# A two-layer hybrid decoder on one core: a fourth pair by seven products in the MLP, low parts and down sums by adding DMAs, the residual kept in HBM, linear attention's products in runs

## The chip, the cores and the metric

One core of one Trainium2 chip runs the whole program. The metric is device time in microseconds, the median of several runs. The engines are TensorE (PE), VectorE (DVE), ScalarE (ACT), GpSimd (POOL) and SyncE (SP), each with its own queue of instructions in a fixed order; 16 DMA engines serve transfers that SP or GpSimd issue.

## The reference

Two layers on x of 256 rows and 2048 columns, all in float32. Each layer is

```python
h = rms_norm(x, attn_norm)
proj = jnp.einsum('bsd,de->bse', h, w_in)
...
mixed = jnp.concatenate([o_gla, o_sb], axis=-1)
x = x + jnp.einsum('bse,ed->bsd', mixed, w_o)
hm = rms_norm(x, mlp_norm)
up = jnp.square(jax.nn.relu(jnp.einsum('bsd,df->bsf', hm, w_up)))
return x + jnp.einsum('bsf,fd->bsd', up, w_down)
```

The projection feeds two groups of heads, eight heads of gated linear attention (`o_gla`) and eight of stick-breaking attention (`o_sb`). The linear attention works on four chunks of 64 rows: per head and chunk there is a state update `u = k_dec^T v` of 64 by 128, scores of 64 by 64 under a causal mask, an output `scores v` within the chunk and `q_e S` from the state of the chunks before. The MLP goes from 2048 to 8192 columns and back.

## The kernel before

**Float32 by three products.** Every weight tile arrives by DMA as `raw`. ScalarE copies it to a rounded high part (`whi`), VectorE subtracts to get the low part (`wlo`), and a float32 product is three matmuls on TensorE: high by high, low weight by high operand, high weight by low operand. Operands have such parts too. A matmul has 512 columns.

**The MLP** (and the output projection and one more column group before it) is cut into units: `g`, two `o`, then for each quarter q of the 8192 columns two `up` units and two `down` units of 1024 output columns each, so 16 MLP units in a layer and 32 in all. A unit has eight pairs j of two k-tiles; one pair is one load of 1 MB (SP, four buffers) and a product of 2 by 2 blocks (two row tiles, two halves of 512 columns, two k-tiles). A plain pair takes eight block products of three matmuls. A pair for which `fast(j)` holds (1, 3 and 5) takes seven, by sums of the weight's blocks (`ts`, `t`, made by VectorE) and of the operand's blocks (`sx`, `sxh`). The products land in eight PSUM banks m: 2, 4, 3 and 8 hold what plain pairs add, 1, 5, 6 and 7 what the seven products add besides. Five high parts and five low parts are in flight (`RING`); the next one in the ring takes the buffer of the one five before.

**Ends of units.** `up_tail` joins the banks, applies relu, turns the result round on TensorE, squares it and makes the operand's parts for the down unit. `down_tail` adds the banks to the residual `xb` in SBUF, twelve steps of 512 columns on VectorE and one copy on ScalarE in each down unit.

**The order.** `Plan` holds pieces with a length, an engine and what they depend on. TensorE's and SP's pieces stay in the order of the code; those of ScalarE and VectorE are sorted by a due time from their users, in a simulated run. The result is a fixed order of each engine.

**Linear attention** (`gla_pair`, `gla_out`) does its small products between the projection's matmuls: state updates (L971, 64 rows of the tile), scores (L988), outputs within the chunk (L1012, 128 rows) and from the state (L1024).

## Time and profile before

| | |
|---|---|
| median of three runs | 2185.33 us (2184.94 to 2186.03) |
| profiled execution | 2184.75 us |
| its span, first to last instruction | 2183.0 us |
| TensorE, VectorE, ScalarE, GpSimd busy | 100%, 85%, 58%, 2% of the span |
| DMA queue of SP | 407 MB, 57.0% of 16 engines |

In the profile's rows the letters after the line number name the engine, `out<-in` the tiles by the program's names; L1263 to L1265 are the three matmuls of one MLP product, L1172 the high parts, L1176 the low parts, L1052 every sum of two tiles on VectorE, L543 to L545 the matmuls of the projection. The attention of the first layer ends at about 300 us, its MLP at about 1070, the second layer has the rest.

### The profile page before, as it was taken

Reading aid. Unit: us, or ns where it says so; the run is one execution under the profiler, and the core shown is the slowest. Engines: PE = TensorE matmul, PEld = TensorE weight load, DVE = VectorE, ACT = ScalarE, POOL = GpSimd, SP = SyncE. Lnnn points to the kernel's source line nnn. Section 1 sums busy time; section 2 is a strip of 40 time slices with the busy share of each in tenths; the row PEclk is TensorE's granted clock in tenths of the full one; section 3 lists DMA queues with packets and bytes.
Section 4 is the critical chain, followed back from the end, with each engine's and each line's share of the span. In section 5 each row is a group of like instructions: output and inputs, shape, how many; then the busy total and the mean of one; then the engine's idle time right before and its main releaser. Section 6 shows DMA issues by size and latency. Waiting matters only on the chain.

```text
span 2183.0 us, 27194 instructions
## 1 busy us (share of the span) xinstructions
PE 2175.0 (100%) x10352; PEld 1803.6 (83%) x10352; DVE 1851.7 (85%) x2394; ACT 1276.6 (58%) x1659; POOL 38.0 (2%) x64
## 2 busy tenths in 40 slices
PE   9999999999999999999999999999999999999999
PEld 7988778888888888888888887788888888888887
DVE  5777568999999999999957775799999999999998
ACT  5555356665566566466556553666665655665663
POOL 0020000000000000000000200000000000000000
PEclk9999999999999999999999999999999999999999
DMA  6644455566556556655546544555656665565564
GB/s 230 198 155 155 154 175 191 164 209 206 193 193 212 185 200 198 208 193 193 174 156 196 171 154 154 174 175 191 214 174 211 199 204 193 193 212 186 199 199 149
DMA packets 144359, 408.98 MB, mean 187 GB/s; under 512 B 6650, under 2 KB 31810, under 8 KB 144228
## 3 DMA queue, kind: packets, MB, share of 16 engines
q1 hardware_dynamic: 144228, 407.24, 57.0%
q8 instruction: 81, 1.33, 0.2%
q14 instruction: 50, 0.41, 0.1%
HBM read 405.12 MB, written 2.10 MB: 187 GB/s over the span
## 4 chain that ended last, share of the span: by engine, by line
PE 99%; DVE 1%; DMA 0%; issue 0%; ACT 0%; SPq 0%; POOL 0%; ACTq 0%
PE acc L543 6%; PE acc L544 6%; PE acc L545 6%; PE acc L590 3%; PE acc L594 1%; PE ps L1012 1%; PE ps L1024 1%; PE ps L971 0%; PE ps L708 0%; PE ps L654 0%; PE ps L672 0%; DVE wlo L1176 0%; PE ps L988 0%; DMA raw<-in_w_in_dram 0%; PE ps L435 0%
## 5 line engine op out<-in xcount | busy, mean ns | idle before, releaser
L1172 ACT ACTIVATE whi<-raw 128x1024 fp32r<-128x1024 f32 x592 | 616.1, 1057 | 349.0 <-ACT whi L1172 11.6
L1176 DVE TENSOR_TENSOR wlo<-raw,whi 128x1024 fp32r<-128x1024 f32 x592 | 715.5, 1218 | 90.9 <-ACT whi L1172 85.7
L526 DVE TENSOR_TENSOR wlo<-raw,whi 128x1024 fp32r<-128x1024 f32 (+2 forms) x194 | 220.1, 1139 | 131.5 <-ACT whi L524 131.1
L524 ACT ACTIVATE whi<-raw 128x1024 fp32r<-128x1024 f32 (+2 forms) x194 | 189.8, 982 | 207.2 <-PE acc L545 158.1
L543 PE MATMUL acc<-whi,act 128*128 128x512 f32 (+2 forms) x640 | 242.3, 379 | 0.4 <-ACT act L445 0.4
L545 PE MATMUL acc<-whi,act 128*128 128x512 f32 (+2 forms) x640 | 237.0, 370 | 0.0
L544 PE MATMUL acc<-wlo,act 128*128 128x512 f32 (+2 forms) x640 | 236.9, 370 | 0.0
L1172 ACT ACTIVATE whi<-t 128x512 fp32r<-128x512 f32 x104 | 65.6, 631 | 162.2 <-DVE t L1052 154.2
L543 PEld LDWEIGHTS acc<-whi,act 128*128 128x128 f32 x640 | 120.9, 189 | 23.2 <-issue 4.1
L545 PEld LDWEIGHTS acc<-whi,act 128*128 128x128 f32 x640 | 120.6, 188 | 20.7 <-DVE act L451 0.2
L544 PEld LDWEIGHTS acc<-wlo,act 128*128 128x128 f32 x640 | 120.8, 189 | 18.9 <-issue 0.7
L1176 DVE TENSOR_TENSOR wlo<-ts,whi 128x1024 fp32r<-128x1024 f32 x104 | 127.1, 1222 | 7.1 <-ACT whi L1172 6.1
L1172 ACT ACTIVATE whi<-ts 128x1024 fp32r<-128x1024 f32 x104 | 109.6, 1054 | 35.1 <-PE m__2487_12202 L1265 2.1
L1052 DVE TENSOR_TENSOR ts<-raw 128x1024 f32<-128x1024 f32 x104 | 126.8, 1219 | 1.4
L590 PE MATMUL acc<-act,whi 128*128 128x512 f32 x256 | 91.9, 402 | 0.0
L1176 DVE TENSOR_TENSOR wlo<-t,whi 128x512 fp32r<-128x512 f32 x104 | 70.9, 682 | 2.8 <-ACT whi L1172 2.8
L594 PE MATMUL acc<-act,wlo 128*128 128x256 f32 x256 | 71.8, 280 | 0.0
L1052 DVE TENSOR_TENSOR raw<-ts,raw 128x512 f32<-128x512 f32 x104 | 70.9, 682 | 0.1
L1052 DVE TENSOR_TENSOR t<-raw 128x512 f32<-128x512 f32 x104 | 70.9, 682 | 0.1
L1349 ACT ACTIVATE act<-act,st 128x512 f32<-128x512 f32 x64 | 44.3, 717 | 26.5 <-DVE act L1052 26.5
L590 PEld LDWEIGHTS acc<-act,whi 128*128 128x128 f32 x256 | 48.1, 188 | 11.1
L594 PEld LDWEIGHTS acc<-act,wlo 128*128 128x128 f32 x256 | 48.4, 189 | 0.1
(2748 smaller groups left out, 5169.2 us busy)
## 6 DMA issues: line engine op xcount, KB each, us to landing
raw<-in_w_up_dram SPq DMA_DIRECT2D x128, 1024.0 KB, 5.0
raw<-in_w_down_dram SPq DMA_DIRECT2D x128, 1024.0 KB, 5.2
raw<-in_w_in_dram SPq DMA_DIRECT2D x84, 1024.0 KB, 5.2
raw<-in_w_o_dram SPq DMA_DIRECT2D x32, 1024.0 KB, 5.3
raw<-in_w_in_dram SPq DMA_DIRECT2D x14, 512.0 KB, 6.5
raw<-in_w_in_dram SPq DMA_DIRECT2D x8, 544.0 KB, 3.8
out_dram<-xb SPq DMA_DIRECT2D x8, 256.0 KB, 3.2
xb<-in_x_dram SPq DMA_DIRECT2D x3, 512.0 KB, 7.9
```

The lines of the kernel that those rows point to most:

```text
L524: newest["hi"] = nc.scalar.activation(h, r, AF.Copy).ins
L526: newest["lo"] = nc.vector.tensor_tensor(lo[:, q : q + step, :width], r, f32(h), ALU.subtract).ins
L543: nc.tensor.matmul(o, xh[:, sl], whi[:, j, :width], start=first, stop=False)
L544: nc.tensor.matmul(o, xh[:, sl], wlo[:, j, :width], start=False, stop=False)
L545: st["mm"] = nc.tensor.matmul(o, xl[:, sl], whi[:, j, :width], start=False, stop=last).ins
L590: nc.tensor.matmul(acc[f], whi[:, j, sl], op.both(k), start=(k == 0), stop=False, skip_group_check=True,)
L594: nc.tensor.matmul(acc[f][:, T:], wlo[:, j, sl], xh, start=False, stop=(k == KT - 1), skip_group_check=True,)
L1012: nc.tensor.matmul(o, sc[:, (2 * tt + j) * P : (2 * tt + j + 1) * P], v[:, tt, vc + j * P : vc + (j + 1) * P], start=first, stop=False, sk ...
L1052: nc.vector.tensor_tensor(dst, a, b, op)
L1172: nc.scalar.activation(box["h"][:, :n], src(), AF.Copy)
L1176: nc.vector.tensor_tensor(box["l"][:, :n], src(), f32(box["h"][:, :n]), ALU.subtract)
L1349: nc.scalar.activation(box[h][:, tt, :], box[h][:, tt, :], AF.Relu, scale=rr[:, tt : tt + 1],)
```

## The change

Four things are changed together.

1. In up and down units four pairs (kind F: 1, 3, 4, 6) go by seven products where there were three; two (kind P: 2, 7) stay plain; two (kind D: 0 and 5) are plain products with the low part made in another way. For D, ScalarE makes the high part of one k-tile (128 by 1024) in a tile `side` and copies it negated into another, and GpSimd issues a DMA that adds the weights from HBM once more to the negated part, which leaves the low part. There are two pairs of `side` tiles. Pair 0 of each layer's first up unit is still made by VectorE.
2. In the down units of the first three quarters the banks are not summed into `xb`: ScalarE copies them, VectorE makes three differences, and GpSimd issues nine DMAs of 256 KB that add the tiles to the residual in HBM, one behind the other where they go to the same columns (`add_tail`).
3. The residual lies in the output tensor in HBM. It is stored after the output projection, loaded into tiles of the activation pool for the last quarter, whose down units sum as before, stored again, and in the second layer loaded on SP at the 20th step of the attention. `side` uses the four residual tiles in the meantime. Masks, a scan's reset row, gate weights and zeroed keys move to a pool of the attention's own and are built again in the second layer.
4. In linear attention the six state products come in one run and the VectorE steps behind them; the four outputs within the chunk come first and then the six from the state.

GpSimd is a fifth engine of the planner, sorted by due times as ScalarE and VectorE are.

```diff
+    KINDS = "DFPFFDFP"
+
     def fast(i):
-        return i in (1, 3, 5)
+        return KINDS[i] == "F"
 
...
             pu = ps_tile()
             S = tmp("S", [P, 3, P], bufs=3)
             for n in range(3):
-                u = pu[:, n * P : (n + 1) * P]
                 for half in range(2):
                     ps = slice(half * DK, (half + 1) * DK)
                     nc.tensor.matmul(
-                        u[ps, :], kdz["t"][:, n, e * P + half * DK : e * P + (half + 1) * DK],
+                        pu[ps, n * P : (n + 1) * P],
+                        kdz["t"][:, n, e * P + half * DK : e * P + (half + 1) * DK],
                         v[:, n // 2, vc + half * P : vc + (half + 1) * P],
                         start=(n == 0), stop=True, skip_group_check=True,
                     )
-                if n == 0:
-                    nc.vector.tensor_copy(S[:, 0, :], u)
-                else:
-                    nc.vector.scalar_tensor_tensor(
-                        S[:, n, :], S[:, n - 1, :], dec[:, e, n : n + 1], u,
-                        ALU.mult, ALU.add,
-                    )
+            nc.vector.tensor_copy(S[:, 0, :], pu[:, :P])
+            for n in range(1, 3):
+                nc.vector.scalar_tensor_tensor(
+                    S[:, n, :], S[:, n - 1, :], dec[:, e, n : n + 1],
+                    pu[:, n * P : (n + 1) * P], ALU.mult, ALU.add,
+                )
...
+            for i, (tt, j) in enumerate((tt, j) for tt in range(NT) for j in range(2)):
+                nc.tensor.matmul(
+                    block(j, tt), sc[:, (2 * tt + j) * P : (2 * tt + j + 1) * P],
+                    v[:, tt, vc + j * P : vc + (j + 1) * P],
+                    start=(i == 0), stop=False, skip_group_check=True,
+                )
+            for n, j in ((1, 0), (2, 0), (1, 1), (2, 1), (3, 0), (3, 1)):
+                tt, half = divmod(n, 2)
+                ps = slice(half * CHUNK, (half + 1) * CHUNK)
+                nc.tensor.matmul(
+                    block(j, tt)[ps, :],
+                    qz[e // 2][:, e % 2, j, n * CHUNK : (n + 1) * CHUNK], S[:, n - 1, :],
+                    start=False, stop=(half == 1), skip_group_check=True,
+                )
...
-        def parts(src, readers, deps, n=2):
-
-            box = {}
-            i = len(whi)
+        def split(src, readers, deps, ring, size, n=2, again=None):
+
+            i = len(ring)
+            box = {"users": []}
 
             def part(tag):
-                if i % RING == 0:
-                    return tmp(tag + "5", [P, 2, 512], F32R, bufs=1)
-                return ppool.tile([P, 2, 512], F32R, tag=tag, name=nm(tag), bufs=RING - 1)
+                if ring is side:
+                    return x_tile(F32R, "side")
+                if i % RING < RING - 4:
+                    return tmp(tag + "5", [P, 2, 512], F32R, bufs=RING - 4)
+                return ppool.tile([P, 2, 512], F32R, tag=tag, name=nm(tag), bufs=4)
 
             def high():
-                box["h"] = part("whi")
+                box["h"], box["l"] = part("whi"), part("wlo")
                 nc.scalar.activation(box["h"][:, :n], src(), AF.Copy)
 
             def low():
-                box["l"] = part("wlo")
                 nc.vector.tensor_tensor(
                     box["l"][:, :n], src(), f32(box["h"][:, :n]), ALU.subtract
                 )
 
-            h = add("ACT", A2 if n == 2 else A1, high, deps, whi[i - RING], last.get("h"))
-            lo = add("DVE", V2 if n == 2 else V1, low, h, wlo[i - RING], last.get("l"))
-            last.update(h=h, l=lo)
-            whi.append([lo])
-            wlo.append([])
-            readers.extend((h, lo))
+            def negated():
+                nc.scalar.activation(box["l"], f32(box["h"]), AF.Copy, scale=-1.0)
+
+            def added():
+                nc.gpsimd.dma_start(box["l"], again, accum_op=ALU.add)
+
+            h = add("ACT", A2 if n == 2 else A1, high, deps, ring[i - size], last.get(size))
+            last[size] = h
+            readers.append(h)
+            if again is None:
+                lo = add("DVE", V2 if n == 2 else V1, low, h)
+                readers.append(lo)
+            else:
+                lo = add("POOL", ADD, added, add("ACT", A2, negated, h), lag=ADD_LAG)
+            box["users"].append(lo)
+            ring.append(box["users"])
             return box, h, lo
+
+        def parts(src, readers, deps, n=2):
+            return split(src, readers, deps, used, RING, n)
...
+            if kind != "o" and KINDS[j] == "D" and (u > 3 or j):
+                if len(side) == SIDE:
+                    side[0].extend(x_read + list(kept.values()))
+                src = weights(u, j)
+                for k in range(2):
+                    made_of = split(
+                        lambda k=k: r()[:, k, :].rearrange("p (c n) -> p c n", c=2),
+                        readers, ld, side, SIDE,
+                        again=src[:, k, :].rearrange("p (c n) -> p c n", c=2),
+                    )
+                    if k == 0:
+                        made_of[0]["more"] = True
+                    yield made_of, [
+                        (m, [(blk(k, tt), c)])
+                        for c, ms in enumerate(((2, 4), (3, 8))) for tt, m in enumerate(ms)
+                    ]
+                return
...
+                if kind == "o":
+                    kept[n] = add(
+                        "POOL", 1.0, lambda: nc.gpsimd.dma_start(columns(n), xb[n]), got, lag=3.5
+                    )
+                    for tt in range(2):
+                        x_last[n, tt] = kept[n]
...
+        def load_back(n):
+            def fn():
+                xb[n] = act_tile(F32, (P, NT, 512))
+                nc.gpsimd.dma_start(xb[n], columns(n))
+
+            p = add("POOL", 1.0, fn, x_last[n, 0], x_last[n, 1], came[-1], lag=4.0)
+            x_last[n, 0] = x_last[n, 1] = p
+
...
+        def add_tail(u):
+            n2 = units[u][2]
+            box = {}
+
+            def into(c, tt, src, *deps):
+                dst = columns(2 * n2 + c, tt)
+                key = (2 * n2 + c, tt)
+                x_last[key] = add(
+                    "POOL", 0.9, lambda: nc.gpsimd.dma_start(dst, src(), accum_op=ALU.add),
+                    *deps, x_last.get(key), lag=3.5,
+                )
+
+            def half_of(name, i):
+                return lambda: box[name][:, i, :]
+
+            def copy(name, i, m):
+                if i == 0:
+                    box[name] = act_tile(F32, (P, 2, 512))
+                nc.scalar.activation(box[name][:, i, :], banks[m], AF.Copy)
+
+            def passing(name, m):
+                box[name] = tmp("t2", [P, 512], bufs=4)
+                nc.scalar.activation(box[name], banks[m], AF.Copy)
+
+            def new_w():
+                box["w"] = act_tile(F32, (P, 2, 512))
+                combine(box["w"][:, 0, :], banks[6], box["c"][:, 0, :], ALU.subtract)
+
+            def sums(p):
+                c1 = add("ACT", A1, lambda: copy("c", 0, 1), p[1])
+                c5 = add("ACT", A1, lambda: copy("c", 1, 5), p[5], c1)
+                w = add("DVE", V1, new_w, c1, p[6])
+                v = vector(half_of("w", 1), bk(7), half_of("w", 0), w, p[7])
+                into(0, 0, half_of("c", 0), c1)
+                into(1, 0, half_of("c", 1), c5)
+                into(1, 1, half_of("c", 1), c5)
+                into(1, 0, half_of("w", 0), w)
+                into(1, 1, half_of("w", 1), v)
+                free.update({1: [c1], 5: [c5], 6: [w], 7: [v]})
+                box["v"] = v
+
+            def half(c, p):
+                if c == 0:
+                    a = add("ACT", A1, lambda: copy("p", 0, 2), p[2])
+                    b = vector(
+                        half_of("p", 1), bk(4), half_of("w", 1), p[4], box["v"], a,
+                        op=ALU.subtract,
+                    )
+                    into(0, 0, half_of("p", 0), a)
+                    into(0, 1, half_of("p", 1), b)
+                    free.update({2: [a], 4: [b]})
+                    return
+                for tt, m in enumerate((3, 8)):
+                    free[m] = [add("ACT", A1, lambda m=m: passing(m, m), p[m])]
+                    into(1, tt, lambda m=m: box[m], free[m])
 
...
             if kind != "g":
-                tails[u] = (up_tail if kind == "up" else down_tail)(u)
+                tails[u] = (
+                    up_tail if kind == "up" else
+                    add_tail if kind == "down" and q < 3 else down_tail
+                )(u)
             begun, p, k = set(), {}, 0
+            if kind == "down" and q == 3:
+                for n in (2 * n2, 2 * n2 + 1):
+                    load_back(n)
             lasts = [j for j in order if j in quick][-1]
             for j in range(4) if kind == "g" else order:
```

**TensorE, linear attention of the first layer.** The rows of the order of before, from the last matmul of the projection ahead of a group (`ps_2284` holds the states' products, `ps_2295` the scores, `ps_2339` the outputs, `S` the states):

```order
L545 MATMUL acc_2265<-whi_2268,act_124 128x512
L971 MATMUL ps_2284<-v_420_2261,kdz_238 64x128 x2
L988 MATMUL ps_2295<-act_1695,act_1817 64x128 x3
L971 MATMUL ps_2284<-v_420_2261,kdz_238 64x128 x2
L988 MATMUL ps_2295<-act_1695,act_1817 64x128
L543 MATMUL acc_2264<-whi_2305,act_134 128x512
...
L971 MATMUL ps_2284<-v_420_2261,kdz_238 64x128 x2
...
L1012 MATMUL ps_2339<-v_420_2261,t_429_2300 128x128
L1024 MATMUL ps_2339<-S_2285,act_1695 64x128
L1012 MATMUL ps_2339<-v_420_2261,t_429_2300 128x128
L1024 MATMUL ps_2339<-S_2285,act_1695 64x128 x2
```

and the same place after the change:

```order
L552 MATMUL acc_2265<-whi_2268,act_120 128x512
L983 MATMUL ps_2284<-v_428_2261,kdz_237 64x128 x6
L1000 MATMUL ps_2295<-act_1695,act_1817 64x128 x4
L550 MATMUL acc_2264<-whi_2305,act_130 128x512
...
L552 MATMUL acc_2265<-whi_2323,act_179 128x512
L1025 MATMUL ps_2339<-v_428_2261,t_437_2300 128x128 x4
L1033 MATMUL ps_2339<-S_2285,act_1695 64x128 x6
L550 MATMUL acc_2264<-whi_2368,act_189 128x512
```

The six state products were in three runs, the last of them behind three matmuls of the projection, and the outputs alternated between the two kinds eight times; now each kind stands in one run.

**ScalarE, the border from the last up unit of a quarter to its first down unit.** Before (the rows of the last two plain pairs, `raw_5266` and `raw_5308`, a bank's copy, and the first two pairs of the next unit):

```order
L1172 ACTIVATE whi_5383<-raw_5266 128x1024
L1172 ACTIVATE whi_1088_5393<-raw_5266 128x1024
L1172 ACTIVATE whi_5398<-raw_5308 128x1024
L1172 ACTIVATE whi_5408<-raw_5308 128x1024
L1326 ACTIVATE act_5417<-m__1057_5248 128x512
L1172 ACTIVATE whi_5428<-raw_1079_5342 128x1024
L1172 ACTIVATE whi_5448<-raw_1079_5342 128x1024
L1172 ACTIVATE whi_1103_5467<-raw_5378 128x1024
```

After, at such a border (`raw_5732` is pair 6, `raw_5808` pair 7, `raw_1221_5861` pair 0 of the down unit):

```order
L1186 ACTIVATE whi_5900<-raw_5732 128x1024
L1186 ACTIVATE whi_5907<-raw_5808 128x1024
L1186 ACTIVATE side_5920<-raw_1221_5861 128x1024
L1186 ACTIVATE whi_5929<-raw_5808 128x1024
L1194 ACTIVATE side_5921<-side_5920 128x1024
L1186 ACTIVATE side_5943<-raw_1221_5861 128x1024
L1447 ACTIVATE act_5954<-m__1189_5723 128x512
L1194 ACTIVATE side_5944<-side_5943 128x1024
L1186 ACTIVATE whi_1244_5967<-raw_5879 128x1024
```

Each k-tile of pair 0 now has two rows, its high part in `side` and the negated copy behind it, and the copies stand behind a high part of pair 7 and behind the copy of a bank.

**TensorE, from pair 6 to pair 0 of the next unit at that border, after the change.** `whi_5849` is the first of pair 6's four high parts, `whi_5907` and `whi_5929` are pair 7's, and `side_5921` is what the DMA has added to:

```order
L1308 MATMUL m__1169_5629<-whi_5849,sxh_3945 128x512
L1306 MATMUL m__1168_5623<-whi_1224_5884,act_3946 128x512
...
L1306 MATMUL m__1165_5615<-whi_5907,act_3812 128x512
...
L1308 MATMUL m__1170_5635<-whi_5929,act_3812 128x512
L1306 MATMUL m__1256_6011<-side_5920,act_5657 128x512
L1307 MATMUL m__1256_6011<-side_5921,act_5657 128x512
```

Between the last matmul that reads `whi_5849` and the first that reads `side_5921` stand 39 matmuls of 512 columns, 15 of pair 6 and 24 of pair 7, and the first of pair 0. `whi_5929` takes the buffer of `whi_5849`.

156 lines of the change are left out of this document (82 added, 74 removed).

## The prediction

> **What bounds the kernel now.** I read the page first, then TensorE's own waits, then stretches of 50 us, and at last single instructions in order of time. The page's span, engine row, queue row and chain:
>
> ```profile
> span 2183.0 us, 27194 instructions
> PE 2175.0 (100%) x10352; PEld 1803.6 (83%) x10352; DVE 1851.7 (85%) x2394; ACT 1276.6 (58%) x1659; POOL 38.0 (2%) x64
> q1 hardware_dynamic: 144228, 407.24, 57.0%
> PE 99%; DVE 1%; DMA 0%; issue 0%; ACT 0%; SPq 0%; POOL 0%; ACTq 0%
> ```
>
> TensorE is the chain (99%). A busy TensorE row alone proves little, because the ends of matmuls are modelled, so the view of waits comes next (engine, line, waited for: us in total, times, longest):
>
> ```profile
> PE ps L493 <- POOL ident masks.py:199: 1.5, 1, 1.5
> PE m__1866_9052 L1264 <- DVE wlo L1176: 0.4, 1, 0.4
> ```
>
> The first is the largest of its waits, the second one of the three in the MLP that there are in all. So a microsecond of matmuls taken away is a microsecond of time, as long as every operand still arrives. Whether it does is the question here. Two stretches of the MLP (start:end, then length, PE, PEld, DVE, ACT, POOL busy, clock, DMA share, GB/s) show the room that the others have:
>
> ```profile
> 600.00:650.00 50.00, 50.00 (x231) 41.53 (x230) 46.59 (x60) 32.94 (x41) 0.00 (x0) 1.00 0.56 190
> 2000.00:2050.00 50.00, 50.00 (x222) 41.43 (x221) 46.80 (x55) 25.41 (x28) 0.00 (x0) 1.00 0.66 224
> ```
>
> VectorE has 3.2 to 3.4 us of 50 left, ScalarE 17 to 25, the DMA engines a third or more, GpSimd everything. The clock is full, so no term below has to allow for it.
>
> **The price of one instruction** is the distance of two starts, not the length of a row, since rows overlap. From the timeline of the MLP (start, length):
>
> ```profile
> 699.86 2.14 ACT L1172 ACTIVATE whi<-raw 128x1024 fp32r<-128x1024 f32 x2
> 699.99 1.23 DVE L1176 TENSOR_TENSOR wlo<-raw,whi 128x1024 fp32r<-128x1024 f32 x1
> 700.06 0.39 PE L1263 MATMUL m__1217_5987<-whi,sx 128*128 128x512 f32 x1
> 700.74 0.39 PE L1263 MATMUL m__1221_5997<-whi,act 128*128 128x512 f32 x1
> 701.13 0.68 DVE L1052 TENSOR_TENSOR xb<-m__1216_5982,xb 128x512 f32<-128x512 f32 x1
> ...
> 712.20 0.68 DVE L1052 TENSOR_TENSOR xb<-m__1201_5920,xb 128x512 f32<-128x512 f32 x1
> 712.80 0.68 DVE L1052 TENSOR_TENSOR xb<-t,xb 128x512 f32<-128x512 f32 x1
> ```
>
> Three matmuls take 0.68 us, 0.2267 each. VectorE's step is 1.14 us for 1024 columns (699.99 to 701.13) and 0.60 for 512 (712.20 to 712.80). ScalarE's is 1.07 for 1024 (2.14 for two); for 512 I take 0.6.
>
> **The change, part by part.**
>
> *Four of eight pairs by seven products.* A pair has eight block products of three matmuls; by seven products it has three matmuls fewer. Each of the 32 units (16 in a layer: up and down, four quarters, two halves) gets one more such pair: 96 matmuls fewer, 96 x 0.2267 = **21.8 us** off TensorE. The rest of the MLP's matmuls stay.
>
> *VectorE in the MLP.* A plain pair costs it two low parts, 2 x 1.14 = 2.28 us; a pair by seven products costs three low parts and one sum of 1024, one low part and two sums of 512: 4 x 1.14 + 3 x 0.60 = 6.36. One plain pair becomes such a pair (+4.08), two plain pairs lose their low parts to DMAs (-4.56). With about +0.7 for the operand's own sums, an up unit stays as it was within 0.2 us while it gets 0.68 shorter: 93% busy becomes about 95. A down unit with drains by DMA keeps 3 of its 12 steps of 0.60 as well, 5.4 us less. VectorE does not become the bound by these sums; it has some 2 us in an up unit as cover, and if that went, the excess would come straight out of the 0.68.
>
> *ScalarE.* The new pair needs about 1.6 us more of high parts; the two pairs with DMAs need high parts by rows and a negated copy of each, four steps where there were two: 2 x 2 x 1.07 = 4.3. In a down unit four more bank copies are added, 2.4. That is 5.9 to 8.3 us in some 42, or 7 to 10 in 50: the busier stretch goes from 33 to 40. Hidden by TensorE, but ScalarE's order now decides when the adding DMAs can start.
>
> *Linear attention's products in runs.* A group now, with the matmuls on both sides of it (each product is two rows of the trace):
>
> ```profile
> 240.08 0.39 PE L545 MATMUL acc<-whi,act 128*128 128x512 f32 x1
> 240.40 0.44 PE L971 MATMUL ps<-v,kdz 128*64 128x128 f32 x4
> 240.66 0.60 PE L988 MATMUL ps<-act,act 128*64 128x128 f32 x6
> 241.23 0.44 PE L971 MATMUL ps<-v,kdz 128*64 128x128 f32 x4
> 241.50 0.38 PE L988 MATMUL ps<-act,act 128*64 128x128 f32 x2
> 241.81 0.50 PE L543 MATMUL acc<-whi,act 128*128 128x512 f32 x1
> 242.15 0.39 PE L544 MATMUL acc<-wlo,act 128*128 128x512 f32 x1
> 242.38 0.40 PE L545 MATMUL acc<-whi,act 128*128 128x512 f32 x1
> 242.71 0.44 PE L971 MATMUL ps<-v,kdz 128*64 128x128 f32 x4
> 243.07 0.50 PE L543 MATMUL acc<-whi,act 128*128 128x512 f32 x1
> 243.41 0.39 PE L544 MATMUL acc<-wlo,act 128*128 128x512 f32 x1
> ...
> 247.76 0.40 PE L545 MATMUL acc<-whi,act 128*128 128x512 f32 x1
> 247.99 0.39 PE L1012 MATMUL ps<-v,t 128*128 128x128 f32 x2
> 248.31 0.43 PE L1024 MATMUL ps<-S,act 128*64 128x128 f32 x2
> 248.67 0.49 PE L1012 MATMUL ps<-v,t 128*128 128x128 f32 x2
> 249.09 0.44 PE L1024 MATMUL ps<-S,act 128*64 128x128 f32 x4
> 249.46 0.49 PE L1012 MATMUL ps<-v,t 128*128 128x128 f32 x2
> ...
> 251.03 0.50 PE L543 MATMUL acc<-whi,act 128*128 128x512 f32 x1
> 251.36 0.40 PE L544 MATMUL acc<-wlo,act 128*128 128x512 f32 x1
> ```
>
> Two rows of L1024 hold TensorE 0.36 us (248.31 to 248.67) and four 0.37 (249.09 to 249.46): what costs is the turn from one kind of tile to another, not the row. States and scores now: 240.08 to 241.81 less one matmul 1.50, 242.38 to 243.07 less one 0.46, and twice 0.11 that the next matmul comes late (0.34 in place of 0.23): 2.18. In runs: twelve rows of L971 at 0.26 / 4, 0.79; eight of L988 at 0.57 / 6, 0.76; a turn in and out, 0.20: 1.75. Saved 0.43. Outputs now: 247.76 to 251.03 less one matmul, 3.04, and 0.11: 3.15. In runs: eight rows of L1012 at 0.08 (0.65), one turn 0.24, twelve of L1024 at 0.055 (0.66), the way out 0.36: 1.9. Saved 1.25. Eight groups (two layers, four each): 8 x 1.68 = **13.4 us**. The weak number is L1012: its second row starts 0.18 after the first (0.49 less one row of 0.31). If 0.18 is the row's own price, the sum is 7; with 0.065 and 0.047 it is 15. I take 0.08, near the runs of L971, whose products are as wide.
>
> *Low parts by adding DMAs.* GpSimd issues four DMAs of 512 KB in a unit, each adding weights from HBM to the negated high part. The trace has no adding DMA. The nearest rows (size, median us from issue to landing):
>
> ```profile
> raw<-in_w_in_dram SPq DMA_DIRECT2D x84, 1024.0 KB, 5.2
> raw<-in_w_in_dram SPq DMA_DIRECT2D x14, 512.0 KB, 6.5
> out_dram<-xb SPq DMA_DIRECT2D x8, 256.0 KB, 3.2
> xb<-in_x_dram SPq DMA_DIRECT2D x3, 512.0 KB, 7.9
> ```
>
> Bounds 3.2 and 7.9. I take 6.2: an add of 512 KB touches 1 MB (5.2), and GpSimd needs some time of its own; the 512 KB rows say 6.5 where queues are deep. What it may take: by the order, where a unit ends ScalarE makes the negated part behind pair 7's second high part, whose buffer is free only when TensorE has left the first of pair 6. From there to the use are 40 matmuls, 9.1 us, less two ScalarE steps, 2.1: **7.0 us** of lead. Counted so over the whole order, 16 places have 7.0, a few 7.7 to 7.9, a dozen 8.6 to 8.9, the rest 9.7 and more. At 6.2 the adds are hidden; that a third of the 16 comes 0.8 late behind a load costs **4 us**. If the cover is gone: 16 us for each us over 7.0, 28 for each over 8.9.
>
> *Down drains and the residual in HBM.* Nine adds of 256 KB in each of 12 down units, in chains of up to three on the same columns, each of which holds GpSimd until the one ahead has landed. Queued behind them on GpSimd are the next unit's low parts of pair 5, which have over 11 us; the first of three can start some 10 us before the unit's end, so nothing is late until an add takes about 11 us. Nil. The residual's stores after the output projection, the loads back for the last quarter and four loads of 512 KB on SP in the second layer stand among loads that run ahead by four buffers: nil, or their few us of transfer if that lead is used up.
>
> *Constants* rebuilt by GpSimd in the second layer end long before the masks are used: nil. The end of the program, the last sums and stores, stays.
>
> **Sum.** Against the profiled execution (2184.75 us, of which 1.75 lie outside the span): 2184.75 - 21.8 - 13.4 + 4 = 2153.6. The median of the runs is 0.6 above that execution, so **2154**.
>
> **Rivals.**
>
> *The adds land late* (slower). At 16 junctions TensorE waits, and as it is the chain, each wait is lost in full. With 35.2 us to lose, it decides from 8.9 + (35.2 - 30.4) / 28 = 9.1 us of landing on. At 10.5 us the loss is 16 x 1.9 + 28 x 1.6 = 75: 2154 - 4 + 75 = 2225. For it: issue by GpSimd and reading the target first are both unseen here, and a loaded queue already shows 7.9. Against: no row is over 7.9.
>
> *The DMA engines become the bound* in down units. What they can move shows at the start, where loads queue:
>
> ```profile
> 12.00:14.00 2.00, 2.00 (x14) 1.82 (x13) 0.48 (x2) 1.35 (x4) 0.00 (x0) 1.00 1.06 401
> ```
>
> A down unit has 8 loads of 1.05 MB, 2.1 MB of low parts and 2.4 MB of drains: 12.9 MB, 32 us at 401 GB/s, under TensorE's 180 x 0.2267 = 40.8. If an add counts twice, since target and source are both read, it is 17.4 MB and 43.4 us: 2.6 us over, 12 units, 31 us, and 2150 + 31 = 2181 or, with the late loads' own stalls, up to 2190. An up unit stays under (12.6 MB, 31 us), so four buffers may carry part of it.
>
> The Trainium skill (Collectives: The Full Stack, the section on the bandwidth ceiling and the fold count) says that an add in the DMA engine costs no cycles but needs two source reads, and so runs at half the rate of a copy. By that rule the second count is the right one and this rival's time holds; no run shown here has an adding DMA, so the trace can't say.
>
> *It doesn't do what it says*: the 96 matmuls are gone in the order, so this can only be the runs, 13.4 us becoming 7: 2160, inside the forecast.
>
> **Chances.** Forecast (2144 to 2175): 0.60. DMA engines (2175 to 2190): 0.12, of which 0.04 end faster, 0.07 within 0.2%, 0.01 slower. Late adds: 0.28, all slower, 0.08 of them under 2196. That is 0.64, 0.07, 0.29; 0.2%, 4.4 us, is about what can be told from no change. The low end is the sum without the 4 and with 15 for the runs, 2148, less the few us of waits that TensorE has now, 2144; the high end, 2196, takes in the DMA case and the mild part of late adds, 0.80 in all.
>
> **What would show it.** Right: 96 matmuls fewer; TensorE's waits under 15 us in all and none on a DMA over 1 us; adds landing under 7 us; the attention's groups about 1.7 and 1.9 us. Wrong: rows of TensorE waiting on DMA for the low parts at unit borders (late adds), or a DMA share near 1 in down units with ScalarE's high parts waiting for loads (DMA engines), or VectorE over 97% with TensorE waiting for low parts.

## The result, and the profile after

The changed kernel takes 2363.43 us (median of four runs, 2361.95 to 2365.09) where the kernel before takes 2185.24 (four runs): 1.0815 times as long, 95% interval 1.0796 to 1.0834. The forecast was 2154, with a range to 2196. The page after, the rows shown of before and the two queues:

```profile
span 2360.1 us, 27633 instructions
PE 2218.2 (94%) x10256; PEld 1813.5 (77%) x10256; DVE 1801.6 (76%) x2370; ACT 1451.4 (61%) x1907; POOL 258.7 (11%) x327
q1 hardware_dynamic: 145316, 409.34, 50.6%
q0 software_dynamic: 36352, 103.83, 22.7%
PE 61%; DMA 22%; issue 8%; ACT 4%; DVE 3%; POOL 1%; SPq 0%; POOLq 0%; ACTq 0%; DVEq 0%
```

The 96 matmuls are gone (10352 to 10256), and yet TensorE is busy for 43 us more and idle for 142 of 2360. A fifth of the chain is DMA now. TensorE's waits (engine, line, waited for: us in total, times, longest):

```profile
PE m__3794_17766 L1307 <- DMA side<-in_w_up_dram: 8.6, 2, 6.6
PE m__1421_6756 L1307 <- DMA side<-in_w_up_dram: 7.5, 2, 5.1
PE m__3053_14457 L1307 <- DMA side<-in_w_down_dram: 7.4, 2, 5.0
```

There are 44 such waits in the view, 124 us in all, on low parts of up and down units alike. The DMA rows (size, median us from issue to landing) say how long those take:

```profile
raw<-in_w_up_dram SPq DMA_DIRECT2D x128, 1024.0 KB, 8.2
raw<-in_w_down_dram SPq DMA_DIRECT2D x128, 1024.0 KB, 7.3
side<-in_w_down_dram POOLq DMA_DIRECT2D x64, 512.0 KB, 10.8
side<-in_w_up_dram POOLq DMA_DIRECT2D x60, 512.0 KB, 9.3
out_dram<-act POOLq DMA_DIRECT2D x92, 256.0 KB, 10.4
out_dram<-t POOLq DMA_DIRECT2D x24, 256.0 KB, 7.9
```

An add of 512 KB takes 9.3 to 10.8 us, and the plain loads beside it 7.3 to 8.2, where before they took 5.0 (up) and 5.2 (down). Four stretches, in the columns of the prediction's windows:

```profile
350.00:400.00 50.00, 50.00 (x231) 41.56 (x230) 46.12 (x62) 32.18 (x46) 1.67 (x2) 1.00 0.68 236
600.00:650.00 50.00, 45.60 (x189) 36.62 (x188) 34.71 (x39) 29.18 (x33) 8.89 (x11) 0.93 0.98 267
2150.00:2200.00 50.00, 41.41 (x174) 33.13 (x175) 35.51 (x38) 27.94 (x33) 11.32 (x13) 0.94 0.99 279
850.00:900.00 50.00, 46.10 (x202) 37.21 (x201) 44.22 (x62) 34.03 (x44) 3.44 (x4) 0.97 0.78 232
```

Only the first, ahead of the first drains, looks like the kernel before. In the next two, with drains, the DMA engines are full (0.98 and 0.99), and the granted clock (the share of full speed that TensorE is given) has left 1.00. The last has adds of low parts but no drains: the engines are at 0.78, as an average, and TensorE waits there too, 3.7 us for one low part. What the clock does shows in the timeline behind one wait (start, length):

```profile
627.75 0.40 PE L1306 MATMUL m__1089_5276<-side,act 128*128 128x512 f32 x1
632.49 0.80 PE L1307 MATMUL m__1089_5276<-side,act 128*128 128x512 f32 x1 [4.34 <-DMA side<-in_w_up_dram]
633.09 0.63 PE L1308 MATMUL m__1089_5276<-side,act 128*128 128x512 f32 x1
633.51 0.63 PE L1306 MATMUL m__1093_5286<-side,act 128*128 128x512 f32 x1
...
636.93 0.60 PE L1308 MATMUL m__1096_5299<-side,act 128*128 128x512 f32 x1
637.35 0.41 PE L1306 MATMUL m__1089_5276<-side,act 128*128 128x512 f32 x1
637.61 0.39 PE L1307 MATMUL m__1089_5276<-side,act 128*128 128x512 f32 x1
```

After 4.34 us without work ten matmuls stand 0.427 us apart (633.09 to 637.35), nearly twice the usual 0.2267, so the wait costs another 2 us. And GpSimd's timeline at the first border of two down units:

```profile
547.39 2.64 POOL L1389 DMA_DIRECT2D out_dram<-act  x3 [1.20 <-ACT act L1399]
557.79 0.86 POOL L1389 DMA_DIRECT2D out_dram<-act  x1 [7.76 <-DMA out_dram<-act]
560.60 0.86 POOL L1389 DMA_DIRECT2D out_dram<-act  x1 [1.94 <-DMA out_dram<-act]
...
571.58 0.86 POOL L1389 DMA_DIRECT2D out_dram<-t  x1 [3.51 <-DMA out_dram<-act]
572.12 2.11 POOL L1197 DMA_DIRECT2D side<-in_w_down_dram  x2
```

A drain is one of the nine adding DMAs of a down unit. The unit's fifth (the first was issued at 544.97) waits 7.76 us for an earlier one, the last is issued at 571.58, and only then pair 5's two low parts.

### The profile page after: what moved, and what is told of

The parts are those of the page before. It is cut to its first block, busy times and chain, and to the rows that moved or that the text cites. A ratio compares the mean times of both kernels' runs of the same rounds, so it can differ in the third digit from the quotient of the medians.

```text
span 2360.1 us, 27633 instructions
## 1 busy us (share of the span) xinstructions
PE 2218.2 (94%) x10256; PEld 1813.5 (77%) x10256; DVE 1801.6 (76%) x2370; ACT 1451.4 (61%) x1907; POOL 258.7 (11%) x327
## 3 DMA queue, kind: packets, MB, share of 16 engines
q1 hardware_dynamic: 145316, 409.34, 50.6%
q0 software_dynamic: 36352, 103.83, 22.7%
## 4 chain that ended last, share of the span: by engine, by line
PE 61%; DMA 22%; issue 8%; ACT 4%; DVE 3%; POOL 1%; SPq 0%; POOLq 0%; ACTq 0%; DVEq 0%
DMA side<-in_w_down_dram 9%; DMA out_dram<-act 6%; PE acc L550 6%; PE acc L552 6%; PE acc L551 6%; DMA side<-in_w_up_dram 4%; PE acc L597 3%; DVE wlo L1189 2%; ACT whi L1186 2%; DMA raw<-in_w_down_dram 2%; PE acc L601 1%; DMA raw<-in_w_up_dram 1%; ACT side L1186 1%; ACT side L1194 1%; POOL out_dram L1389 1%
## 5 line engine op out<-in xcount | busy, mean ns | idle before, releaser
L1189 DVE TENSOR_TENSOR wlo<-raw,whi 128x1024 fp32r<-128x1024 f32 x468 | 562.3, 1219 | 194.7 <-ACT whi L1186 193.3
L1186 ACT ACTIVATE whi<-raw 128x1024 fp32r<-128x1024 f32 x468 | 483.6, 1052 | 199.9 <-PE m__3388_15951 L1308 14.7
L1063 DVE TENSOR_TENSOR ts<-raw 128x1024 f32<-128x1024 f32 x136 | 165.8, 1219 | 37.2 <-DMA raw<-in_w_up_dram 20.9
L1189 DVE TENSOR_TENSOR wlo<-ts,whi 128x1024 fp32r<-128x1024 f32 x136 | 166.2, 1222 | 34.1 <-ACT whi L1186 33.5
L1186 ACT ACTIVATE side<-raw 128x1024 fp32r<-128x1024 f32 x124 | 130.3, 1051 | 96.9 <-DMA raw<-in_w_up_dram 28.5
L1186 ACT ACTIVATE whi<-ts 128x1024 fp32r<-128x1024 f32 x136 | 142.7, 1049 | 8.9 <-PE m__597_3024 L1308 2.1
L1194 ACT ACTIVATE side<-side 128x1024 fp32r<-128x1024 f32 x124 | 130.2, 1050 | 1.1
L1197 POOL DMA_DIRECT2D side<-in_w_down_dram x64 | 56.8, 908 | 555.5 <-ACT side L1194 481.7
L1197 POOL DMA_DIRECT2D side<-in_w_up_dram x60 | 54.1, 968 | 515.8 <-ACT side L1194 447.0
L1389 POOL DMA_DIRECT2D out_dram<-act x84 | 75.1, 977 | 156.4 <-DMA out_dram<-act 116.3
## 6 DMA issues: line engine op xcount, KB each, us to landing
side<-in_w_down_dram POOLq DMA_DIRECT2D x64, 512.0 KB, 10.8
out_dram<-act POOLq DMA_DIRECT2D x92, 256.0 KB, 10.4
```

The source lines that it names most:

```text
L1063: nc.vector.tensor_tensor(dst, a, b, op)
L1186: nc.scalar.activation(box["h"][:, :n], src(), AF.Copy)
L1189: nc.vector.tensor_tensor(box["l"][:, :n], src(), f32(box["h"][:, :n]), ALU.subtract)
L1194: nc.scalar.activation(box["l"], f32(box["h"]), AF.Copy, scale=-1.0)
L1197: nc.gpsimd.dma_start(box["l"], again, accum_op=ALU.add)
L1389: "POOL", 0.9, lambda: nc.gpsimd.dma_start(dst, src(), accum_op=ALU.add),
```

## The experiments

The theory after the result: an add costs the DMA engines much more than a copy; in down units they have more work than time, so low parts and loads land late, and behind the longer waits matmuls run at half the rate. Rivals: GpSimd's queue (the drains hold the low parts), too little lead in the order, and costs that have nothing to do with adds. "Left out" says what a kernel does not compute. From e11 on, all but e12 are the changed kernel with e5's constant and one edit (e18 and e19: two), against 2357.

### The parts alone

**e1: the attention's runs in the kernel before.**

```diff
-  state product, its VectorE step (three times); outputs block by block
+  six state products in one run, then the VectorE steps;
+  four outputs within the chunk, then six from the state
```

> The kernel before with linear attention's products in runs and nothing else. Theory 1 (the prediction's term): 8 groups by 1.68 us, 13.4 us less, 2172; TensorE's waits stay as before. Theory 2 (a row of the outputs within the chunk costs 0.18 us in itself): 7 us less, 2178. If the runs cost something elsewhere (the state's chain on VectorE now starts later), nothing or a loss, 2185 or more, with TensorE waiting for the states.

2170.30, ratio 0.9933 (0.9919 to 0.9946): 15.2 us off. The groups as runs:

```profile
240.45 0.39 PE L545 MATMUL acc<-whi,act 128*128 128x512 f32 x1
240.77 0.88 PE L970 MATMUL ps<-v,kdz 128*64 128x128 f32 x12
241.48 0.61 PE L987 MATMUL ps<-act,act 128*64 128x128 f32 x8
242.01 0.50 PE L543 MATMUL acc<-whi,act 128*128 128x512 f32 x1
```

From 240.45 to 242.01 less one matmul is 1.33, and 0.11 that the next one comes late: 1.44, where the prediction had 1.75. This part is sound, and it alone beats both kernels.

**e2, e3, e4: no drains' adds, no low parts' adds, neither.** Left out: the drained sums; the low parts of kind D; both.

```diff
-  add("POOL", 0.9, lambda: nc.gpsimd.dma_start(dst, src(), accum_op=ALU.add), ...)
+  add("POOL", 0.9, None, ...)                            # e2, e4
-  lo = add("POOL", ADD, added, ...)
+  lo = add("POOL", ADD, None, ...)                       # e3, e4
```

> The changed kernel without the nine adding DMAs of each down unit (the copies and differences are made and then left, so the output lacks them); the low parts' adds stay. Theory L (an add takes 8 us or more by itself beside the loads, and the lead is too short): most waits on low parts stay, 2230 to 2300. Theory Q (the drains are the cause: their chains hold GpSimd, and behind them stand the low parts of pair 5): the waits at pair 5 vanish, adds land under 7.5 us, 2150 to 2185. Theory B (DMA engines full in down units): the share of about 0.97 in down units falls to about 0.75, and the time to 2150 to 2185 as well.

> The changed kernel without the adding DMAs of the low parts (what stands in the low tile is the negated high part, so the output is not the reference's); the drains stay. No instruction of TensorE waits for a drain. Theory L and Q: 2150 to 2160, drains land in 5 to 7 us. Theory B: loads of weights still land late in down units, 2165 or more, with ScalarE and VectorE waiting for loads.

> The changed kernel without either kind of adding DMA; every instruction of TensorE, VectorE and ScalarE is there. If the prediction's first terms hold (96 matmuls and the runs, with VectorE and ScalarE covered), 2148 to 2152 and a clock of 1.00 throughout. Rival: VectorE or ScalarE is late without any DMA's help, 2165 or more.

2290.78 (ratio 1.0482, 1.0463 to 1.0501), 2178.97 (0.9974, 0.9961 to 0.9987) and 2176.96 (0.9962, 0.9947 to 0.9977). Against e4, low parts alone cost 114 us, drains alone 2 (no more than the spread of the runs), both 186: some 70 us come only from the two together. And e4 stands 27 us over the 2150 that the prediction's sum gives without adds; TensorE waits for no DMA there but x at the start.

**e5: e4 and a constant of 24 bytes more** (left out as in e4).

```diff
   gqk = cpool.tile([P, DEPTH], F32, name="gqk")
+  cpool.tile([P, 6], F32, name="pad")
```

> The run without either kind of adding DMA again, with one more tile of 24 bytes a partition among the constants, so that the tiles behind them (the side tiles too) start on another address. In that run a matmul that reads a side tile takes 0.2333 us and every other MLP matmul 0.2267; 1488 such matmuls are 10 us. Theory A (the address that the constants leave, 2088 bytes, is what costs): 0.2267 for all, 2167. Theory S (it is something else about the side tiles): 0.2333 as before, 2177.

2164.03 (0.9905, 0.9889 to 0.9922): 13 us off. The same product's matmuls from the `side` tiles, first in e4, then in e5:

```profile
706.67 0.40 PE L1306 MATMUL m__1342_6356<-side,act 128*128 128x512 f32 x1
...
708.78 0.40 PE L1306 MATMUL m__1350_6377<-side,act 128*128 128x512 f32 x1
```

```profile
704.21 0.39 PE L1307 MATMUL m__1342_6357<-side,act 128*128 128x512 f32 x1
...
706.25 0.39 PE L1307 MATMUL m__1350_6378<-side,act 128*128 128x512 f32 x1
```

Nine matmuls take 2.11 us in e4, 0.234 each, and 2.04 in e5, 0.2267. There are 1488 of them: 11.6 us. The constants take 2088 bytes of a partition, 8 over a multiple of 32, and 2112 with the new one. That the tile's start address is what counts is the reading of it; no other size was tried.

**e10: e1 and the same constant.**

> The kernel before, with the linear attention's products in runs and a 24-byte constant more. Theory: the address cost in e4 sat on the tiles that only the changed kernel has (side), all other moving tiles of the kernel before read at 0.2267 us already, so the constant does nothing here or shifts something else off its place: 2170 as without it if the first, 2180 to 2195 if it puts the streamed weights off (some 3000 matmuls by 0.0066 is 20 us). Rival: the kernel before has the same 8 bytes somewhere too, and gains: 2155 to 2165.

2171.13 (0.9934, 0.9921 to 0.9948), as without it: nothing in the kernel before gains by the move, so the cost came with the changed kernel. That fits the `side` tiles.

**e11: the changed kernel and the same constant.**

> The changed kernel as it is, with a 24-byte constant more. Theory: the two costs add where TensorE works and do not where it waits; of the 13 us that the constant saved without the adds, most come back: 2345 to 2358. Rival: where TensorE waits for adds anyway, faster matmuls only make the waits longer: 2358 to 2366.

2357.04 (1.0783, 1.0764 to 1.0803), 6 us off: part comes back, part only makes waits longer. TensorE is busy 2211.8 us in e11 and 2146.5 in e5, with the same 10256 matmuls. So of the 194 us between their spans (2358.1 and 2164.0) 129 are idle and 65 lie in TensorE's rows; some 215 matmuls that stand about 0.43 us apart make some 43 of these.

### The add, the lead, the engine

**e6: e2 with plain copies for the low parts** (left out: the drained sums; the low parts hold the weights themselves).

```diff
-  nc.gpsimd.dma_start(box["l"], again, accum_op=ALU.add)
+  nc.gpsimd.dma_start(box["l"], again)
```

> The changed kernel without the drains' adds, and with the low parts' DMAs as plain copies of the same weights into the same tiles (nothing is added, so the output is not the reference's). Against the run without drains' adds, 2290.8, where adds land in 8.7 (up) and 10.5 us (down). Theory D (the add is slow because the DMA engine reads source and target): copies land in 5 to 6.5 us, 2177 to 2200. Theory G (GpSimd's way of issuing, or sharing the engines with the loads, is what is slow): copies land in 8 us or more too, 2260 to 2290.

2187.34 (1.0012, 1.0002 to 1.0023): of the 114 us, 103 are the add's. GpSimd's queue (packets, MB, share of 16 engines) in e4, then with landings in e2 and e6:

```profile
q0 software_dynamic: 2944, 10.49, 1.3%
```

```profile
q0 software_dynamic: 20800, 75.51, 16.6%
side<-in_w_down_dram POOLq DMA_DIRECT2D x64, 512.0 KB, 10.5
side<-in_w_up_dram POOLq DMA_DIRECT2D x60, 512.0 KB, 8.7
```

```profile
q0 software_dynamic: 20800, 75.51, 10.2%
side<-in_w_down_dram POOLq DMA_DIRECT2D x64, 512.0 KB, 7.1
side<-in_w_up_dram POOLq DMA_DIRECT2D x60, 512.0 KB, 5.2
```

The same packets and bytes. By the spans (2287.7, 2183.5, and 2175.2 of e4) an add takes (379.8 - 28.3) / 124 = 2.83 us of all 16 engines, a copy (222.7 - 28.3) / 124 = 1.57: 1.8 times. The Trainium skill (Collectives: The Full Stack, the section on the bandwidth ceiling and the fold count) puts the add of a ring's ReduceScatter at half the rate of a copy, for its two source reads; the 1.8 here is near that.

**e7: e2 with pairs D F F P D F F P and the add's lag told as 9.5** (left out as in e2), and **e9: e7 without low parts' adds**.

```diff
-  KINDS = "DFPFFDFP"
+  KINDS = "DFFPDFFP"
-  ADD, ADD_LAG = 1.2, 4.5
+  ADD, ADD_LAG = 1.2, 9.5
```

> The changed kernel without the drains' adds, with the pairs in the order DFFPDFFP, so that three pairs stand between any two pairs of kind D, and with 9.5 us in place of 4.5 in the planner for the landing of a low part's add; by the order the lead is then 9 to 16 us, most above 10, where it was 7 to 12. Theory L (the adds of low parts cost only because they land after their lead): 2177 to 2200, clock near 1.00. Theory B (the DMA engines have no room for them however early they start): still 2230 or more, and loads of weights late.

> The kernel of e7 (order of the pairs D F F P D F F P, low parts asked for 9.5 us ahead) without the low parts' adds; the low parts' content of the four-product pairs is left out, as is that of the drains. The control for e7's 2249. If e7's remaining loss is the DMA engines' (adds slow the loads of weights, the high parts come late): about what e4 took, 2175 to 2182, and TensorE waits for no load. If it is the new order's own (VectorE's sums of two seven-product pairs stand behind each other): 2210 or more, and e7's comparison with e2 says little about lead. In between, the difference to e4's 2177 is the order's share.

2249.06 (1.0295, 1.0274 to 1.0315) and 2186.18 (1.0001, 0.9991 to 1.0011). The new order itself costs 9 us (e9 against e4). With more lead TensorE waits for none of the added low parts in e7, yet the adds still cost 63 us over e9. ScalarE's waits in e7 show where:

```profile
ACT whi L1186 <- DMA raw<-in_w_down_dram: 60.3, 20, 5.8
ACT whi L1186 <- DMA raw<-in_w_up_dram: 43.1, 21, 3.9
```

High parts wait for plain loads, which land after 7.8 (up) and 8.5 us (down) there, and after 5.0 and 5.1 in e9, without adds. So too little lead is worth some 50 of the 114, and the rest goes, as far as these waits show it, through the loads.

**e8: the changed kernel with D's low parts by VectorE.**

```diff
-  again=src[:, k, :].rearrange("p (c n) -> p c n", c=2),
+  again=None,
```

> The changed kernel with the low parts of the D pairs made by VectorE as before the change, the drains' adds kept. The sum for VectorE in an up unit is 39.9 + 4.6 = 44.5 us beside 42.6 on TensorE, so if VectorE's sums are right it becomes the bound there: 1.9 us in 16 units on top of 2179, 2205 to 2220. If its steps are cheaper than I counted, 2180 to 2190, and then the adding DMAs were not needed for the fourth pair.

2226.01 (1.0189, 1.0169 to 1.0209):

```profile
PE 2175.7 (98%) x10256; PEld 1777.2 (80%) x10256; DVE 1928.1 (87%) x2494; ACT 1322.9 (59%) x1783; POOL 151.0 (7%) x203
```

That is over the expected range. TensorE waits 42 us in e8, 34 of them for VectorE, though that is busy 87% on average. In this kernel, with its drains by DMA, the fourth pair does not pay when VectorE makes all low parts either.

### The seventy that come only together

**e12: e11 with e7's order and lag, and adds for low parts in up units alone** (VectorE makes the others).

> The changed kernel with the 24-byte constant, the order D F F P D F F P, low parts asked for 9.5 us ahead, and adds for low parts in the up units alone (in the down units VectorE makes them); the drains still add. Theory (low parts' adds and drains' adds hurt most by meeting in the down units, on GpSimd's queue and on the DMA engines): kept apart they cost little: 2185 to 2205, the rest VectorE's in the down units. Rival (each add costs its own, wherever): half of e7's 80 us over the kernel without adds, and VectorE's half of e8's: 2215 to 2240.

2314.58 (1.0589, 1.0570 to 1.0609): over both expectations. So this edit does not part them. An up unit's first adds run beside the drains of the down unit ahead of it, and its second pair's stand behind those drains in GpSimd's timeline:

```profile
604.87 0.86 POOL L1390 DMA_DIRECT2D out_dram<-t  x1 [5.64 <-issue]
607.69 0.86 POOL L1390 DMA_DIRECT2D out_dram<-t  x1 [1.96 <-DMA out_dram<-act]
608.23 2.11 POOL L1198 DMA_DIRECT2D side<-in_w_up_dram  x2
```

TensorE waits 42 us for VectorE's low parts, 28 for ScalarE and 26 for adds. What each of the two is worth was not parted.

**e17: the drains to places of their own** (left out: the sum of the three buffers).

```diff
-  dst = columns(2 * n2 + c, tt)
+  dst = columns(n, tt) if not turn else av[turn - 1][:, tt, n * 512 : (n + 1) * 512]
```

> The changed kernel with the 24-byte constant, where the first drain to a place adds to it as before and the second and third add to two buffers of their own in HBM (filled once with x at the start; the three are never summed, which is left out). As many adds, of as many bytes, none waits for another of its unit. If the 77 us are the chain's in GpSimd's queue: 2280 to 2305. If they are the engines': 2340 to 2360.

2362.03 (1.0808, 1.0768 to 1.0848). At the start TensorE waits 11.9 us for x behind the filling of the buffers, 0.6 in the changed kernel; less those 11 it is some 2351, 6 under e11, with 7 us between its own two runs. GpSimd's timeline at the same border:

```profile
559.95 2.32 POOL L1397 DMA_DIRECT2D apart<-act  x2
561.70 3.24 POOL L1397 DMA_DIRECT2D out_dram<-act  x3
...
571.83 0.86 POOL L1397 DMA_DIRECT2D apart<-t  x1 [1.84 <-DMA out_dram<-act]
580.66 0.87 POOL L1203 DMA_DIRECT2D side<-in_w_down_dram  x1 [7.98 <-PE m__1013_4937 L1314]
```

The low part is held by its tile now (released by TensorE), no longer by drains. But the drains, all in flight at once, take 16 to 18 us each, and TensorE waits for low parts 112 us in all (124 in the changed kernel, 130 in e11). The chain in the queue is there, but is worth some 6 us of 193.

**e13: the drains write instead of adding** (left out: all of each sum but its last term).

```diff
-  nc.gpsimd.dma_start(dst, src(), accum_op=ALU.add)
+  nc.gpsimd.dma_start(dst, src())
```

> The changed kernel with the 24-byte constant (2357), where the drains write instead of adding; so the output holds only the last term of each sum. Order, chain of waits and bytes written stay; each drain reads once instead of twice. If the 77 us that drains and low parts cost only together are the DMA engines' (the second read): 2278 to 2300, near the kernel without drains (2291, less the constant's 13). If they are the chain's in GpSimd's queue: the links get shorter, not fewer; with 8 us falling to 4 to 6, 2300 to 2335.

2295.53 (1.0504, 1.0473 to 1.0534): 62 us off, with the same order and the same chain.

```profile
q0 software_dynamic: 29440, 103.83, 19.8%
```

By the spans a drain takes (535.7 - 379.8) / 108 = 1.44 us of all engines as an add and (453.9 - 379.8) / 108 = 0.69 as a write. Its adds also have 6912 packets more (36352 in the changed kernel), so here the factor of 2.1 need not be the second read alone.

**e14: plain copies for the low parts, drains add** (low parts hold the weights). **e18: the same, drains apart as in e17. e19: e13, drains apart.**

> The changed kernel with the 24-byte constant, where the low parts are plain copies (their content is then the weights', not the low parts) and the drains add. Plain copies without drains cost 10 us over no copies (2187 against 2177). If the loss needs slow adds of low parts, on the engines: 2176 to 2195. If the drains' chain in the queue holds whatever comes behind it: the copies of pair 5 and pair 0 land as late as before, and 2225 to 2260.

> e14 (low parts as plain copies, drains add) with the drains to separate places as in e17. Filling the two buffers holds the start for some 11 us, as in e17. If the 57 us that adding drains cost beside copies are the chain's in GpSimd's queue: 2185 to 2205. If they are the time that the drains' adds take on the DMA engines: 2232 to 2250.

> e13 (low parts add, drains write) with the drains to separate places as in e17, 11 us of filling at the start included. If the some 17 us that writing drains cost beside adding low parts (2295 against 2291 less the constant's 13) are the chain's: 2282 to 2294. If the engines': 2300 to 2315.

2231.43 (1.0210, 1.0181 to 1.0240), 2229.90 (1.0203, 1.0173 to 1.0233) and 2302.84 (1.0537, 1.0503 to 1.0570). e14 came out as the chain's theory had it, 57 us over copies without drains (2187.34 less the constant's 13). e18 contradicts that reading: without the chain, and less the 11 us of filling, some 2219. So 12 of the 57 are the chain's and 45 stay. e19, less the same 11, is 2292, 4 under e13. With e17, the chain is worth 4 to 12 us in all three; only the 12 is clear of the spread of the runs.

**e15: the planner told 10 us for each add and drain.**

```diff
-  ADD, ADD_LAG = 1.2, 4.5      # and lag=3.5 of a drain
+  ADD, ADD_LAG = 1.2, 10.0     # and lag=10.0
```

> The changed kernel with the 24-byte constant, and the planner told that a low part's add and a drain take 10 us (4.5 and 3.5 before). The low parts' adds are asked for as early as their two tiles allow, and pair 5's second pair of adds goes ahead of the last two drains of the unit in GpSimd's order. If late asking and the queue carry most of the loss: 2300 to 2325. If the tiles and the DMA engines set it: 2340 to 2360.

2369.16 (1.0841, 1.0809 to 1.0872), over both expectations and 12 us worse. At the border shown above pair 5's low parts are issued at 568.46 and 571.82 (both at 574.26 in e11), ahead of the last two drains, and TensorE, which waits 4.6 us for them in e11, no longer does. But for pair 0's, which stand among the first drains, it waits 6.1 us (3.0 in e11): the wait moves and does not go. In the whole kernel it waits 120 us for low parts (130), while its rows take 12 us more (2224.2 against 2211.8).

**What this settles.** That these transfers add, and not that they are there, is the main cause: plain copies take 103 of the 114 us of the low parts away (e6), and plain writes take 62 of the drains' (e13). The chain is a small cause (e17 to e19). The order's lead is worth some 50 without drains (e7), but a longer lag brings no time back once drains add too (e15).

How an add's time turns into lateness is shown in part. A down unit has eight loads of 1.05 MB (the queue of loads moved 409.34 MB in 50.6% of 2360.1 us, 3.06 us a load), four adds of 2.83 us and nine drains of 1.44: 24.5 + 11.3 + 13.0 = 48.8 us of all 16 engines, an estimate from averages, under 180 matmuls of 40.8. Without drains' adds it is 35.8, with writing drains 42.0, with copied low parts and adding drains 43.8. That fits the full engines in down units (0.98 and 0.99 above), and the two kinds costing together what neither costs alone.

It does not explain e2, which loses 114 us at 35.8. From 550 to 600 us its DMA share is 0.80, near the 0.78 of the changed kernel's stretch without drains, and TensorE waits 3.1 us there for one low part; stretches of 4 us in it go from 0.07 to 1.05. So without drains the engines have room on average, and the adds, with the loads beside them, are late all the same. How much of that is the length of one add and how much its queueing with loads was not parted, nor, for the changed kernel, how much of a low part's lateness comes from its load. TensorE's own waits there name low parts for 124 of 136 us.

## Why the prediction was wrong

The step that failed is the pricing of the adding DMAs: 4 us for the low parts and nothing for the drains. The low parts' adds alone cost 114 us (e2 against e4), and the drains, which alone cost 2, cost 73 more on top of them.

- **The 96 matmuls** left TensorE, as said. But with all adds out and with the constant (e5), the kernel gains 21 us on the kernel before, and e1 has 15.2 of them: the fourth pair is worth 6, not 21.8. TensorE is idle 17.5 us in e5 and 8.6 in e1, 9.3 of it waiting for VectorE (low parts, sums at the ends of up units). So "VectorE does not become the bound" failed at such places, though its share of the whole fell. Some 8 us more lie in rows of TensorE and stay open.
- **The attention's runs**: 15.2 for 13.4, the one term that held. Its two halves were off in opposite ways, so the nearness of the total is in part luck: states and scores take 1.44 (1.75 forecast), the outputs 2.11 (1.9; in e1's timeline from 247.37 to 249.60 less one matmul, and the same 0.11).
- **The low parts' landing** is the term that failed worst. The 6.2 us came from rows of plain transfers; the measured 8.7 (up) and 10.5 (down) in e2, without drains, lie over the upper bound of 7.9, and the 10.5 is over the lead at every place counted as short (7.0 to 8.9). The sentence "an add of 512 KB touches 1 MB" had the second read, but took it from a row in a queue without other adds.
- **"28 per us over 8.9", each wait "lost in full"**: the late-adds rival gave 2225 at 10.5 us. e2 has those landings and takes 2291. The waits on low parts there are 77 us, about the rival's 75. What it lacked are the slow matmuls behind the waits: TensorE's rows take 2194.3 us in e2 and 2157.7 in e4, 37 more, and 77 and 37 make the 114.
- **"Nothing late until an add takes about 11 us"** for the drains: a drain took 7.9 to 10.4 us, under that bound, and the low parts of pair 5 were late all the same. The drains' "nil" is the second term that failed. The bound weighed the queue and not the engines. With the queue free of the chain (e17) the time is 6 us better, no more.
- **The rival of the DMA engines** had the mechanism of the down units, at 0.12, and its sign, a share near 1, is there: it counted 43.4 us of engine time in a down unit and took the excess of 2.6 as the loss. The runs give about 48.8, and transfers are late long before the sum passes TensorE's 40.8 (e2: 35.8 us a unit, and 114 us lost). So the sum alone, even with the right prices, would not have given 2363.
- **ScalarE, constants, residual**: none of TensorE's waits on them is over 1.5 us. But moving the tiles put `side` where reading it costs 13 us, which no row of before could show.

## What to carry to other kernels

Price an adding DMA at about two copies of the engines' time (1.8 and 2.1 here), and sum that per stage against what the loads take there; then ask whether each one lands in time, since e2 lost its time with room on the engines on average. When a kernel's TensorE is full, a late operand costs more than its wait: here 1 to 2.4 us came on top of each wait over 3 us (5 to 12 matmuls that each take 0.2 us more). Where several edits come together, run each alone: here the runs of linear attention, the smallest, are the only one of which a gain worth keeping was shown.

## What the runs showed of the hardware

**The clock falls after short waits.** In the timeline of the changed kernel's MLPs all 20 waits over 3 us are followed by 5 to 12 matmuls about 0.427 us apart; of ten between 2.15 and 2.7 us, six are, as behind this one, and four are not; none under 2 is.

```profile
753.68 0.80 PE L1307 MATMUL m__1342_6405<-side,act 128*128 128x512 f32 x1 [2.22 <-DMA side<-in_w_down_dram]
754.27 0.63 PE L1308 MATMUL m__1342_6405<-side,act 128*128 128x512 f32 x1
754.70 0.63 PE L1306 MATMUL m__1345_6413<-side,act 128*128 128x512 f32 x1
```

The Trainium skill (TensorE: Matmul & The Clock Gate, the part on the HAM clock gate) has TensorE at half rate after an idle window of about 3.4 us that runs freely, and at full rate again after about as long of work. The 0.427 us agrees with its half rate; that 2.2 us can be enough is shorter than the page says. The wait shown begins some 1.3 us behind the slow matmuls of another one (4.11 us, ended at 747.09); one of 2.28 us that ends at 1629.24, with none over 1 us in the 13 us before it, is followed by five.

**Moving a tile by 24 bytes** took 3% off the matmuls that read it (0.234 against 0.2267 us, e4 and e5). What about the old place cost them was not tested.
